# Squares added on VectorE, three pairs on x not yet normed in every layer, and output products seven pairs behind

## The chip, the core and the metric

The kernel runs on one core of a Trainium2 chip. Its time is what the device takes for one execution, in microseconds (us); 1053.85 is the median of three runs (1053.67 to 1056.78). The core has TensorE (PE, matrix products into PSUM), VectorE (DVE), ScalarE (ACT), GpSimd (POOL) and SyncE (SP, which here issues the loads of the weights).

## The reference

Two stacks of layers in float32 on a sequence of 256 positions and 1024 features. Every layer is x = x + f(norm(x)), where norm is

```
y = x32 * lax.rsqrt(jnp.mean(x32 * x32, axis=-1, keepdims=True) + EPS)
return (y * g.astype(jnp.float32)).astype(x.dtype)
```

The layers in their order: mixer0 (attention and pooling), ffn0, mixer1 (a gated linear recurrence), ffn1, mixer2 (four branches on quarters of the features: rwkv, spatial gating, a short convolution and s5, a complex diagonal recurrence), ffn2, and a last norm. ffn0 and ffn1 are

```
z = causal_dwconv(h @ w_in, conv_w, conv_b)
u, g = jnp.split(z, 2, axis=-1)
return (jax.nn.gelu(g) * u) @ w_out
```

with 2816 features in u and in g. In mixer2 and ffn2 the normed x is also scaled and shifted by factors computed from a second input.

## The kernel before

x is kept transposed in SBUF as eight tiles X[m] of 128 features by 256 positions. A weight is 128x128; each product with one takes three matmuls of 256 columns in the fp32r format, high by high, high by low and low by high (lines 281 to 283 in `mm3`, line 286 in the norm products). The weights come in chunks of 16 by SP's DMAs (`raw`). Half a chunk, eight weights or 24 matmuls, is one split: ScalarE casts the high half (`hi`, line 247) and VectorE subtracts it for the low half (`lo`, line 323). Splits are made up to four ahead, in five buffers each for hi and lo, and beyond these in slots borrowed from an arena of 46.

The order of the instructions on each engine comes from a list scheduler at build time, which takes the program's text, in three lanes, and starts what it believes ready; each engine runs its own list in order. Where the text moves a step, the scheduler may move others.

Ahead of each layer stands a norm. The last product of the layer before (`out_last`) finishes X[m] one tile after the other; `norm_add` squares each on ScalarE and adds the squares up. `norm_sum` sums over the features with two matmuls of one column and starts the reciprocal square root, some twelve tiny operations on VectorE (the tiles nv, nr...y, nr...t). `norm_spread` spreads the result over the partitions by two more matmuls, and `make_h` writes the normed tiles hs.

PE doesn't wait for that: `in_gen` starts the layer's first pairs of column tiles on x that has only the norm's gain on it (`xgh`, high, and `xgl`, low, the latter being the group s<-xp,pvt,xgh of the trace) and multiplies the result by the norm's factor afterwards. A pair is two weight columns, u and g of ffn, with eight steps of k. The function `products` issues them, and its second argument says at which of the eight steps the sum and the spread stand. Later pairs use hs.

`ffn` takes its 22 pairs from `in_gen`; `evac` of a pair has ScalarE and VectorE do the convolution, the gelu, the product and its split, and `out(k)` adds pair k's output product to X's accumulators, LAG pairs behind. The last four pairs go through `out_last`. In s5 (`s5_run`), eight parts p pass through st_a (rotation, with two adds on GpSimd), st_b (two scans and a rotation back on VectorE) and st_c (the products with C), which are taken in groups of four; PE does other branches of mixer2 between them.

Of the kernel before, what the change touches and what calls it, by code (L numbers as in the profile page):

```python
# [11 lines left out]
AF = mybir.ActivationFunctionType  # L12
OP = mybir.AluOpType
# [3 lines left out]
T = 256  # L17
# [9 lines left out]
N_CHUNK = -(-N_TILES // TPC)  # L27
N_SLOT = 46
MAGIC = 12582912.0
NORM_A, NORM_B = 4, 6  # L30
SUM_AT, SPREAD_AT = 6, 1
SB = 3
SC = 6
STEPS0 = (3, 7)
# [7 lines left out]
S5_N = 4  # L42
S5_W = (2, 5, 8)
RW_W = 1
LAG = 5
LAST = 4
LAG2 = 3
LAST2 = 2
# [89 lines left out]
class Prog:  # L138
# [226 lines left out]
    def norm_add(self, m):  # L365
        nc = self.nc
        acc = self.sacc[:, :T]
        if self.gain is not None:
            self.split_act(self.X[:, m, :], *self.xgo(m), scale=self.gain(m))
        if self.nsq == 0:  # L370
            nc.scalar.activation(acc, self.X[:, m, :], AF.Square)
        elif self.nsq < 7:
            sq = self.sqb[:, (self.nsq % 2) * T:(self.nsq % 2) * T + T]
            nc.scalar.activation(sq, self.X[:, m, :], AF.Square)  # L374
            nc.gpsimd.tensor_tensor(acc, acc, sq, op=OP.add)  # L375
        else:
            sq = self.sqb[:, T:]
            nc.scalar.activation(sq, self.X[:, m, :], AF.Square)  # L378
            self.tt(acc, acc, sq, OP.add)
        self.nsq += 1  # L380
# [421 lines left out]
    def in_gen(self, specs, hs, scaled=False):  # L802

        lead = 0 if hs else 3 if self.shift is not None else 2
        if lead:
            sh = self.shift is not None
            n = T + 2 if sh else T  # L810
            bs, o = [], []

            def products(js, at):

                for j in js:
                    b = [self.bk() for _ in range(2 if sh else 1)]
                    bs.append(b)
                    o.append([x[:, :n] for x in b] if sh else [b[0][:, :T], b[0][:, T:]])
                for q, k in enumerate(self.ORDER):
                    if q in at:  # L820
                        at[q]()
                    xh, xl = self.xgo(k, n)
                    for j in js:
                        for i, (w, m) in enumerate(specs[j]):
                            wh, wl = self.W((w, k, m))
                            self.mm(o[j][i], wh, xh, q == 0 and (sh or i == 0), False)
                            self.mm(o[j][i][:, :T], wh, xl, False, False)
                            self.mm(o[j][i], wl, xh, False, q == KD - 1)
            rbs = []

            def spread():
                rbs.append(self.norm_spread())
                if not scaled:
                    hs.extend(self.make_h(rbs[0]))
            if sh:
                products((0, 1), {SUM_AT: self.norm_sum})
                products((2,), {SPREAD_AT: spread})
            else:
                products((0, 1), {NORM_A: self.norm_sum, NORM_B: spread})
            rb = rbs[0]  # L840
            if not scaled:
                self.fr(*self.xgl)
            self.set_lead(4, self.down)
            for j in range(lead):
                z = self.al()
                if sh:
                    bias = self.cst([128, 2], f"hb{self.uid}")
                    for i in range(len(specs[j])):
                        zi = z[:, i * T:i * T + T]
                        self.tt(zi, o[j][i][:, :T], rb[:, :T], OP.mult)  # L850
                        self.nc.vector.tensor_reduce(bias[:, i:i + 1], o[j][i][:, T:n], axis=AX.X, op=OP.add)
                        self.nc.scalar.activation(zi, zi, AF.Identity, bias=bias[:, i:i + 1])
                else:
                    b = bs[j][0]
                    self.tt(z.rearrange("p (i t) -> p i t", i=2), b.rearrange("p (i t) -> p i t", i=2),
                            rb[:, :T].unsqueeze(1).to_broadcast([128, 2, T]), OP.mult)
                self.bf(*bs[j])
                if j == lead - 1 and not scaled:
                    self.fr(rb)
                yield j, z  # L860
        for j in range(lead, len(specs)):
            b = self.bk()
            for k in range(KD):
                for i, (n, m) in enumerate(specs[j]):
                    x = self.xgo(k) if scaled else self.hl(hs[k])
                    self.mm3(b[:, i * T:i * T + T], (n, k, m), x, k == 0 and i == 0, k == KD - 1)
                if k == 3:
                    self.step()
            if scaled:
                z = self.al()  # L870
                self.tt(z.rearrange("p (i t) -> p i t", i=2), b.rearrange("p (i t) -> p i t", i=2),
                        rb[:, :T].unsqueeze(1).to_broadcast([128, 2, T]), OP.mult)
                self.bf(b)
                b = z
            yield j, b
        if scaled:
            self.fr(rb, *self.xgl)


    def ffn(self, l):  # L880
# [24 lines left out]
        def out(k):  # L905
            if k == 0:
                self.acc_begin()
            self.out_k(wo, k, self.hl(ys[k]), k == 0)
            self.fr(ys.pop(k))
        for p, b in self.in_gen(specs, hs):  # L910
# [3 lines left out]
            if p == SIDE:  # L914
                self.lanes[1].append((self.rg_small, self.s5_setup)[l]())
            if p >= LAG and p - LAG < NFT - LAST:
                out(p - LAG)
        self.fr(*hs)
        if l == 1:
# [3 lines left out]
            self.ts(self.gt1h, self.mod[:, 16:24], 0.5, OP.mult)  # L923
        for k in range(NFT - LAG, NFT - LAST):
            out(k)
# [271 lines left out]
    def s5_run(self, ud):  # L1197

        nc = self.nc
# [46 lines left out]
        def st_c(ps):  # L1246


            for n, (c, q, i) in enumerate(((0, 0, 0), (1, 0, 1), (1, 1, 0), (0, 1, 1))):
                for p in ps:  # L1250
                    r = 32 * (p % 4)
                    self.mm(yb[r:r + 32, (p // 4) * T:(p // 4) * T + T], self.s5c[:, c, p, :], Y[p][q][:, i, :],
                            n == 0, n == 3)
            for p in ps:
                self.fr(*Y.pop(p))

        for s in range(8 + S5_C):
            if s >= S5_C and (s - S5_C) % S5_N == S5_N - 1:
                st_c(range(s - S5_C - S5_N + 1, s - S5_C + 1))
            if 0 <= s - 1 < 8:  # L1260
                Y[s - 1] = st_b(s - 1, V.pop(s - 1))
            if s < 8:
                V[s] = st_a(s)
            yield
            if s in S5_W:
                yield
# [725 lines left out]
```

## Time and profile before

| | |
|---|---|
| median of three runs | 1053.85 us |
| the profiled execution | 1055.76 us |
| its span | 1054.0 us, granted clock 0.988 |
| PE busy | 1022.2 us, 97% |
| VectorE busy | 865.2 us, 82% |
| ScalarE busy | 609.1 us, 58% |
| GpSimd busy | 130.2 us, 12% |
| read from HBM | 200.32 MB, 191 GB/s over the span |

A row of the timeline gives the start of an instruction, its duration, the engine, the line of the kernel, the operation, output<-inputs by the program's names, the shapes, the count where equal neighbours are drawn together, and in brackets the idle time of the engine in front and the instruction that ended it. A row of the windows gives, for a stretch of time, each engine's busy time and instruction count. The page is the summary of the whole execution.

### The profile page before, as it was taken

Reading aid. Unit: us, or ns where it says so; the run is one execution under the profiler, and the core shown is the slowest. Engines: PE = TensorE matmul, PEld = TensorE weight load, DVE = VectorE, ACT = ScalarE, POOL = GpSimd, SP = SyncE. Lnnn points to the kernel's source line nnn. Section 1 sums busy time; section 2 is a strip of 40 time slices with the busy share of each in tenths; the row PEclk is TensorE's granted clock in tenths of the full one; section 3 lists DMA queues with packets and bytes.
Section 4 is the critical chain, followed back from the end, with each engine's and each line's share of the span. In section 5 each row is a group of like instructions: output and inputs, shape, how many; then the busy total and the mean of one; then the engine's idle time right before and its main releaser. Section 6 shows DMA issues by size and latency. Waiting matters only on the chain. (4 is left out here: it accounts for less than half of the span.)

```text
span 1054.0 us, 21535 instructions
## 1 busy us (share of the span) xinstructions
PE 1022.2 (97%) x8834; PEld 988.3 (94%) x8834; DVE 865.2 (82%) x1616; ACT 609.1 (58%) x953; POOL 130.2 (12%) x128
## 2 busy tenths in 40 slices
PE   9999999999989999999999999889999999999996
PEld 8878999999989999999998999778999999999996
DVE  5887899987789989999999887998567979775553
ACT  6556665555669966665654588223335557444444
POOL 2001000000010011000394200244300220000001
PEclk9999999999999999999999999989999999999999
DMA  8952467976572183678546544224445454955531
GB/s 306 351 184 83 158 215 276 321 267 222 192 268 90 44 294 123 229 255 293 204 160 199 191 161 147 94 81 161 161 153 209 158 168 159 381 178 197 179 142 41
DMA packets 32499, 202.76 MB, mean 192 GB/s; under 512 B 3600, under 2 KB 5136, under 8 KB 9232
## 3 DMA queue, kind: packets, MB, share of 16 engines
q1 hardware_dynamic: 31392, 199.80, 53.8%
q10 hardware_dynamic: 1008, 1.58, 0.5%
q8 instruction: 69, 1.13, 0.4%
q14 instruction: 30, 0.25, 0.1%
HBM read 200.32 MB, written 1.05 MB: 191 GB/s over the span
## 5 line engine op out<-in xcount | busy, mean ns | idle before, releaser
L282 PE MATMUL b<-s,hi 128*128 128x256 f32 x2248 | 636.2, 283 | 1.7 <-DVE s L332 0.9
L281 PE MATMUL b<-s,hi 128*128 128x256 f32 x2172 | 615.8, 285 | 4.8 <-ACT s L343 2.5
L283 PE MATMUL b<-s,lo 128*128 128x256 f32 x2172 | 612.7, 283 | 1.4 <-DVE lo L323 1.4
L323 DVE TENSOR_TENSOR lo<-raw,hi 128x1024 fp32r<-128x1024 f32 (+1 forms) x311 | 391.6, 1264 | 113.5 <-ACT hi L247 113.0
L247 ACT CAST hi<-raw 128x1024 fp32r<-128x1024 f32 (+1 forms) x311 | 322.5, 1041 | 276.6 <-PE b L282 251.4
L282 PEld LDWEIGHTS b<-s,hi 128*128 128x128 f32 x2248 | 426.2, 190 | 6.2 <-issue 3.1
L281 PEld LDWEIGHTS b<-s,hi 128*128 128x128 f32 x2172 | 411.0, 190 | 12.5 <-issue 3.5
L283 PEld LDWEIGHTS b<-s,lo 128*128 128x128 f32 x2172 | 411.6, 190 | 2.9 <-DVE lo L323 1.8
L375 POOL TENSOR_TENSOR s<-s,s 128x256 f32<-128x256 f32 x42 | 38.2, 910 | 595.9 <-ACT s L374 592.8
L332 DVE SCALAR_TENSOR_TENSOR s<-b,pvt,s 128x255 f32<-128x255 f32 (+1 forms) x161 | 75.9, 476 | 2.2 <-ACT s L889 1.0
L323 DVE TENSOR_TENSOR s<-s,s 128x256 fp32r<-128x256 f32 (+3 forms) x131 | 72.3, 563 | 2.0 <-ACT s L378 0.6
L466 DVE SCALAR_TENSOR_TENSOR ada<-ada,s 128x512 f32<-128x512 f32 x96 | 63.6, 682 | 2.1 <-DMA ada<-in_ada_dram 2.1
L286 PE MATMUL b<-xgh,hi 128*128 128x258 f32 (+1 forms) x172 | 50.2, 292 | 0.0
L889 ACT ACTIVATE s<-b,pvt 128x256 f32<-128x256 f32 x80 | 43.8, 555 | 10.5 <-PE b L283 10.4
L286 PE MATMUL b<-xgh,lo 128*128 128x258 f32 (+1 forms) x172 | 49.9, 290 | 0.0
L286 PE MATMUL b<-s,hi 128*128 128x256 f32 x172 | 49.7, 289 | 0.0
L343 ACT CAST s<-s 128x256 fp32r<-128x256 f32 (+1 forms) x77 | 32.8, 439 | 27.6 <-DVE s L323 19.1
L286 PE MATMUL b<-s,s 128*32 128x256 f32 (+5 forms) x204 | 35.5, 353 | 6.3 <-DVE s L323 5.9
L323 DVE TENSOR_TENSOR s<-s 128x256 f32<-128x256 f32 (+3 forms) x70 | 35.5, 508 | 4.5 <-ACT s L1798 4.0
L286 PEld LDWEIGHTS b<-s,s 128*32 128x32 f32 (+3 forms) x204 | 21.5, 151 | 13.6 <-issue 8.2
L286 PEld LDWEIGHTS b<-s,hi 128*128 128x128 f32 x172 | 34.0, 198 | 0.0
L286 PEld LDWEIGHTS b<-xgh,lo 128*128 128x128 f32 x172 | 33.9, 197 | 0.0
(370 smaller groups left out, 1047.3 us busy)
## 6 DMA issues: line engine op xcount, KB each, us to landing
raw<-in_wst_dram SPq DMA_DIRECT2D x157, 1024.0 KB, 5.0
ada<-in_ada_dram SPq DMA_DIRECT2D x24, 1024.0 KB, 7.2
raw<-in_wst_dram SPq DMA_DIRECT2D x4, 512.0 KB, 7.0
s<-in_catt_dram SPq DMA_DIRECT2D x8, 192.0 KB, 6.9
s<-in_rgw_dram SPq DMA_DIRECT2D x5, 256.0 KB, 2.7
raw<-in_wst_dram SPq DMA_DIRECT2D x4, 256.0 KB, 5.6
xp<-in_xt_dram ACTq DMA_DIRECT2D x3, 256.0 KB, 6.4
s<-in_cinv_dram SPq DMA_DIRECT2D x2, 256.0 KB, 5.8
```

The costliest lines, as they stand in the source:

```text
L247: self.nc.scalar.copy(h, s)
L281: mm(out, wh, x[0], start=start, stop=False, skip_group_check=True)
L282: mm(out, wh, x[1], start=False, stop=False, skip_group_check=True)
L283: mm(out, wl, x[0], start=False, stop=stop, skip_group_check=True)
L286: self.nc.tensor.matmul(out, l, r, start=start, stop=stop, skip_group_check=True)
L323: self.nc.vector.tensor_tensor(out, a, b, op=op)
L332: self.nc.vector.scalar_tensor_tensor(out, a, s, b, op0=op0, op1=op1)
L343: nc.scalar.copy(hi, src)
L375: nc.gpsimd.tensor_tensor(acc, acc, sq, op=OP.add)
L466: self.nc.vector.scalar_tensor_tensor(x, x, 0.5, self.cs[h], op0=OP.mult, op1=OP.mult, accum_out=self.macc[:, h, i:i + 1])
L889: nc.scalar.activation(c[:, i, :], z, AF.Identity, scale=self.pv(f"fcw{l}2", m), bias=self.pv(f"fcb{l}", m))
```

## The change

1. `norm_add`: every square after the first is added by VectorE. Before, GpSimd added the second to the seventh, and VectorE the eighth.
2. `in_gen`: three pairs go on x not yet normed in the unshifted layers too (ffn0, mixer1, ffn1), where it was two. The sum stands at step 6 of the first two pairs and the spread at step 2 of the third; before, they stood at steps 4 and 6 of the first two. In the shifted layers (mixer2, ffn2) the spread moves from step 1 to step 2.
3. `ffn`: LAG 5 becomes 7.
4. `s5_run`: one more `yield` ahead of each group of C products.

```diff
-NORM_A, NORM_B = 4, 6
-SUM_AT, SPREAD_AT = 6, 1
+SUM_AT, SPREAD_AT = 6, 2
...
-LAG = 5
+LAG = 7
...
-        elif self.nsq < 7:
+        else:
             sq = self.sqb[:, (self.nsq % 2) * T:(self.nsq % 2) * T + T]
-            nc.scalar.activation(sq, self.X[:, m, :], AF.Square)
-            nc.gpsimd.tensor_tensor(acc, acc, sq, op=OP.add)
-        else:
-            sq = self.sqb[:, T:]
             nc.scalar.activation(sq, self.X[:, m, :], AF.Square)
             self.tt(acc, acc, sq, OP.add)
...
-        lead = 0 if hs else 3 if self.shift is not None else 2
+        lead = 0 if hs else 3
...
-            if sh:
-                products((0, 1), {SUM_AT: self.norm_sum})
-                products((2,), {SPREAD_AT: spread})
-            else:
-                products((0, 1), {NORM_A: self.norm_sum, NORM_B: spread})
+            products((0, 1), {SUM_AT: self.norm_sum})
+            products((2,), {SPREAD_AT: spread})
...
             if s >= S5_C and (s - S5_C) % S5_N == S5_N - 1:
+                yield
                 st_c(range(s - S5_C - S5_N + 1, s - S5_C + 1))
```

On PE, ahead of ffn0, the sum (b<-cb,s) stood before the change inside the products with the split hi_1185:

```order
L286 MATMUL b_130_1285<-xgh,hi_1185 128x256
L286 MATMUL b_130_1285<-s_128_1128,hi_1185 128x256
L286 MATMUL b_130_1285<-xgh,lo_1186 128x256
L286 MATMUL b_131_1344<-cb,s_123_1123 128x1 x2
L286 MATMUL b_129_1284<-xgh,hi_1185 128x256
L286 MATMUL b_129_1284<-s_125_1125,hi_1185 128x256
```

and with the change it stands here:

```order
L285 MATMUL b_130_1285<-xgh,hi_1223 128x256
L285 MATMUL b_130_1285<-s_126_1126,hi_1223 128x256
L285 MATMUL b_130_1285<-xgh,lo_1224 128x256
L285 MATMUL b_131_1374<-cb,s_123_1123 128x1 x2
L285 MATMUL b_129_1284<-xgh,hi_1223 128x256
L285 MATMUL b_129_1284<-s_127_1127,hi_1223 128x256
```

It has moved behind one more split of weights (hi_1223 follows hi_1185), 24 matmuls, the products of one step having 12. The spread follows 36 matmuls after the sum, where it followed after 32.

On VectorE, at the end of ffn1, the last pair's evacuation (s_444, and its split into s_445) and the weight splits (lo) stood in this order:

```order
L323 TENSOR_TENSOR lo_7192<-raw_7023,hi_7191 128x1024
L332 SCALAR_TENSOR_TENSOR s_444_7207<-b_443_7142,pvt,s_444_7207 128x255
L332 SCALAR_TENSOR_TENSOR s_444_7207<-b_443_7142,pvt,s_444_7207 128x254
L323 TENSOR_TENSOR lo_7232<-raw_7023,hi_7231 128x1024
L332 SCALAR_TENSOR_TENSOR s_444_7207<-b_443_7142,pvt,s_444_7207 128x255
L332 SCALAR_TENSOR_TENSOR s_444_7207<-b_443_7142,pvt,s_444_7207 128x254
L323 TENSOR_TENSOR s_444_7207<-s_444_7207 128x256
L323 TENSOR_TENSOR lo_7268<-raw_7088,hi_7267 128x1024
L323 TENSOR_TENSOR s_445_7216<-s_444_7207,s_445_7216 128x256
L323 TENSOR_TENSOR xp<-xp,b_390_5448 128x256
```

With the change, where the same pair is s_454 and s_455:

```order
L322 TENSOR_TENSOR lo_7140<-raw_6971,hi_7139 128x1024
L331 SCALAR_TENSOR_TENSOR s_454_7155<-b_453_7090,pvt,s_454_7155 128x255
L331 SCALAR_TENSOR_TENSOR s_454_7155<-b_453_7090,pvt,s_454_7155 128x254
L322 TENSOR_TENSOR lo_7180<-raw_6971,hi_7179 128x1024
L331 SCALAR_TENSOR_TENSOR s_454_7155<-b_453_7090,pvt,s_454_7155 128x255
L331 SCALAR_TENSOR_TENSOR s_454_7155<-b_453_7090,pvt,s_454_7155 128x254
L322 TENSOR_TENSOR s_454_7155<-s_454_7155 128x256
L322 TENSOR_TENSOR lo_7216<-raw_7036,hi_7215 128x1024
L322 TENSOR_TENSOR s_455_7164<-s_454_7155,s_455_7164 128x256
L322 TENSOR_TENSOR lo_7244<-raw_7036,hi_7243 128x1024
L322 TENSOR_TENSOR lo_7274<-raw_7107,hi_7273 128x1024
L322 TENSOR_TENSOR xp<-xp,b_406_5630 128x256
```

The weight splits ahead of the last split are fewer against what PE still has to do: after it, two more of them follow before X is added to (xp<-xp,b), where X followed at once.

On PE, in s5's second group, the first C products (32x256, s_564, s_568 and s_578 being the parts 4, 5 and 6) stood apart:

```order
L283 MATMUL b_589_8755<-s_471_7616,lo_8636 128x256
L286 MATMUL b_530_8341<-s_564_8554,s_387_5389 32x256
L286 MATMUL b_530_8341<-s_568_8611,s_387_5389 32x256
L281 MATMUL b_591_8832<-s_526_8300,hi_8635 128x256
L282 MATMUL b_591_8832<-s_527_8301,hi_8635 128x256
L283 MATMUL b_591_8832<-s_526_8300,lo_8636 128x256
...
L281 MATMUL b_591_8832<-s_526_8300,hi_8635 128x256
L286 MATMUL b_530_8341<-s_578_8678,s_387_5389 32x256
L282 MATMUL b_591_8832<-s_527_8301,hi_8635 128x256
```

With the change the three (s_574, s_581, s_588) stand together:

```order
L281 MATMUL b_602_8843<-s_477_7630,hi_8677 128x256
L282 MATMUL b_602_8843<-s_477_7630,lo_8678 128x256
L285 MATMUL b_540_8353<-s_574_8566,s_397_5401 32x256
L285 MATMUL b_540_8353<-s_581_8640,s_397_5401 32x256
L285 MATMUL b_540_8353<-s_588_8718,s_397_5401 32x256
L280 MATMUL b_602_8843<-s_478_7631,hi_8727 128x256
L281 MATMUL b_602_8843<-s_478_7631,hi_8727 128x256
```

Part 6's product has moved 24 to 26 matmuls to the back; those of the parts 4 and 5 come up to it. In the first group the parts 0 and 1 come up to part 2 in the same way, and part 2 stands two rows later than it did.

## Rows read from the trace of the kernel before

**Rows 1.** Page, busy time of each engine: us, share of the span, instructions
```profile
PE 1022.2 (97%) x8834; PEld 988.3 (94%) x8834; DVE 865.2 (82%) x1616; ACT 609.1 (58%) x953; POOL 130.2 (12%) x128
```

**Rows 2.** Waits of PE: us in total, times, longest us
```profile
PE b L286 <- DVE s L323: 11.8, 5, 3.0
...
PE b L283 <- DVE lo L323: 1.4, 2, 1.0
```

**Rows 3.** Busy time by stretch; us, PE PEld DVE ACT POOL, then PEclk, DMA share, GB/s
```profile
120.00:185.00 65.00, 65.00 (x550) 64.91 (x550) 64.77 (x161) 42.44 (x69) 0.00 (x0) 1.00 0.62 219
...
410.00:515.00 105.00, 104.85 (x887) 104.65 (x887) 104.25 (x260) 66.97 (x105) 0.54 (x3) 1.00 0.67 235
580.00:590.00 10.00, 10.00 (x78) 10.00 (x78) 8.12 (x12) 6.52 (x13) 3.12 (x4) 0.89 0.33 112
```

**Rows 4.** Timeline of PE at the three sums: start, us, [idle before <-releaser]
```profile
108.31 0.28 PE L286 MATMUL b<-s,hi 128*128 128x256 f32 x1
108.43 0.28 PE L286 MATMUL b<-xgh,lo 128*128 128x256 f32 x1
110.42 0.58 PE L286 MATMUL b<-cb,s 128*128 128x1 f32 x4 [1.71 <-DVE s L323]
...
111.25 0.42 PE L286 MATMUL b<-xgh,lo 128*128 128x256 f32 x1
111.46 0.42 PE L286 MATMUL b<-xgh,hi 128*128 128x256 f32 x1
...
114.59 0.28 PE L286 MATMUL b<-xgh,hi 128*128 128x256 f32 x1
...
305.26 0.70 PE L286 MATMUL b<-cb,s 128*128 128x1 f32 x4 [2.77 <-DVE s L323]
...
402.43 0.58 PE L286 MATMUL b<-cb,s 128*128 128x1 f32 x4 [1.48 <-DVE s L323]
```

**Rows 5.** Timeline of DVE at the norm ahead of ffn0
```profile
97.51 2.25 DVE L332 SCALAR_TENSOR_TENSOR s<-xp,pvt,xgh 128x256 fp32r<-128x256 f32 x3
...
101.48 0.96 DVE L332 SCALAR_TENSOR_TENSOR s<-xp,pvt,xgh 128x256 fp32r<-128x256 f32 x1
102.36 1.76 DVE L323 TENSOR_TENSOR lo<-raw,hi 128x1024 fp32r<-128x1024 f32 x1
104.05 0.47 DVE L332 SCALAR_TENSOR_TENSOR s<-xp,pvt,xgh 128x256 fp32r<-128x256 f32 x1
...
106.24 1.84 DVE L332 SCALAR_TENSOR_TENSOR s<-xp,pvt,xgh 128x256 fp32r<-128x256 f32 x2
...
109.87 0.41 DVE L323 TENSOR_TENSOR s<-s,s 128x256 f32<-128x256 f32 x1
110.23 1.22 DVE L323 TENSOR_TENSOR lo<-raw,hi 128x1024 fp32r<-128x1024 f32 x1
```

**Rows 6.** Page, the squares' adds on GpSimd: xcount | busy, mean ns | idle before
```profile
L375 POOL TENSOR_TENSOR s<-s,s 128x256 f32<-128x256 f32 x42 | 38.2, 910 | 595.9 <-ACT s L374 592.8
```

**Rows 7.** Timeline of PE at ffn1's end
```profile
577.46 0.39 PE L281 MATMUL b<-s,hi 128*128 128x256 f32 x1 [1.65 <-ACT s L343]
578.49 0.42 PE L282 MATMUL b<-s,hi 128*128 128x256 f32 x1 [0.65 <-DVE s L323]
```

**Rows 8.** Timeline of DVE at the same place
```profile
578.02 0.42 DVE L323 TENSOR_TENSOR s<-s,s 128x256 fp32r<-128x256 f32 x1
```

**Rows 9.** Timeline of PE in s5, at the two late C products
```profile
684.03 0.59 PE L286 MATMUL b<-s,s 128*32 128x256 f32 x2 [3.04 <-DVE s L323]
...
708.15 0.79 PE L286 MATMUL b<-s,s 128*32 128x256 f32 x2 [2.81 <-DVE s L323]
```

**Rows 10.** Timeline of DVE in s5, two scans that follow each other
```profile
705.31 1.78 DVE L1238 TENSOR_TENSOR_SCAN s<-s5mag,s 128x256 f32<-128x256 f32 x2 [0.63 <-POOL s L1229]
...
711.30 1.78 DVE L1238 TENSOR_TENSOR_SCAN s<-s5mag,s 128x256 f32<-128x256 f32 x2
```

**Rows 11.** Timeline of PE at the spread ahead of ffn2
```profile
872.08 0.49 PE L286 MATMUL b<-cb,nr709y 128*128 128x128 f32 x2 [0.98 <-DVE nr709y L332]
```

## The prediction

> **What bounds the kernel now.** I read the page first [rows 1]: TensorE (PE) is busy for 1022.2 of 1054.0 us, VectorE (DVE) for 865.2. A matmul of 256 columns starts every 0.12 us when nothing is late (108.31, 108.43 in [rows 4]), so the matmuls are the floor, and a change can win only where PE stands still or runs at a lower clock. PE's waits come next [rows 2]: 11.8 us of them are five waits for one operation of VectorE, while the low halves of split weights (lo) cost 1.4 us in all. The timeline says where these are: the norm's sum of squares ahead of the first feed-forward layer (ffn0), of mixer1 and of ffn1 [rows 4], and two C products in s5 [rows 9]. Two more waits stand at ffn1's end [rows 7] and one at ffn2's spread [rows 11].
>
> Most of these waits cost more than themselves. Behind the 1.71 us at 110.42, matmuls start 0.21 us apart (111.25, 111.46) instead of 0.12, until 114.59 [rows 4]: the half clock, 1.2 for 2.4 GHz. 16 matmuls take 3.34 us there instead of 1.9, so the dip costs about 1.5 us with the two matmuls before. The granted clock of 0.89 behind ffn1's end [rows 3] shows one more. I price a dip at 1.5 us wherever a wait of 1.7 us or more goes, and none for the 1.48 at 402.43, behind which the stretch of 410 to 515 us has a clock of 1.00.
>
> Last comes VectorE where the sums wait for it [rows 5]. The split of the gained x (s<-xp,pvt,xgh) takes 0.47 us alone (104.05), and 0.96 (101.48) while GpSimd adds squares; a lo takes 1.22 alone (110.23) and 1.76 beside such an add (102.36). Over the six adds ahead of ffn0 that is 2.25 for some 1.27 in the three at 97.51, 0.49 at 101.48, 0.54 at 102.36 and 1.84 for some 0.87 in the two at 106.24: 3.0 us that VectorE loses to GpSimd. So it is VectorE, itself held up by GpSimd, that the sum waits for.
>
> **The change part by part.** *Squares on VectorE.* 42 adds of 0.91 us leave GpSimd [rows 6], and 42 come to VectorE. One such add takes 0.41 us, 0.36 from start to start (109.87 to 110.23) [rows 5]; I take 0.34 in a dense run, so 2.0 us a norm. Against 3.0 us of stretching that goes, VectorE has 1.0 us less to do ahead of a sum (0.9 taken) in the five norms with xgl; the first and the last norm have no such splits and gain nothing there. I cost those two at 0 (between +1 and −1 us): the first starts among the loads, and the last trades six adds of 0.91 for shorter ones just before the end. Each add stands behind its square on ScalarE; the xgl split of about half a us before it in VectorE's queue covers most of that wait, and what is queued behind an add is the next lo.
>
> The Trainium skill (SBUF — State Buffer, "Who interferes with whom") says that a VectorE instruction with two inputs in SBUF and a GpSimd instruction that reads SBUF exclude each other for the whole instruction. The trace agrees that they collide, but the stretch is about 0.5 us an instruction, not the 0.91 us of an add. By the rule the six adds would cost up to 5.5 us, and VectorE would gain 3.5 a norm; the sum would change by mixer1's 0.2 alone, since the other waits at the sums are gone by either. The skill (Perfetto Trace Analysis, "Optimizing Scalar/DVE Operations") also advises offloading a saturated VectorE, even to GpSimd, which is the reverse of this edit, while warning that the two share a port. Here the warning fits the rows better than the advice; what the advice would make of it is the last rival.
>
> *Late sum, three pairs.* In the order for PE the sum stands 24 matmuls later in ffn0 and ffn1, 2.8 us at 0.118 each, and 13 later in mixer1, 1.5 us. With 0.9 less on VectorE, ffn0's wait of 1.71 goes (3.7 us of room against 1.7), and its dip: −3.2. ffn1's 1.48 goes: −1.5. Mixer1's 2.77 is met by 1.5 + 0.9 = 2.4, so 0.2 to 0.4 may stay, too short for a dip: 2.77 + 1.5 − 0.2 = −4.1. What is late next is the spread: it stands 36 matmuls behind the sum in ffn0 and ffn1, 4.2 us, and 60 in mixer1, 7.1 us. The chain between is one short add, some eleven tiny operations and a lo, about 4.5 us in ffn0 from the sum's end, against 4.7 with the sum itself; up to 0.5 us may be late, which goes to the new waits below. For mixer2 and ffn2 the spread stands 4 to 7 matmuls later: ffn2's wait of 0.98 [rows 11] loses 0.8 by that and 0.9 by VectorE: −0.7 taken, between −1.0 and 0.
>
> *Seven pairs behind.* At ffn1's end PE waits 1.65 us for a split on ScalarE and 0.65 for the low half made by VectorE at 578.02 [rows 7, 8], the last pair's evacuation, and runs at half clock behind it. With two more pairs of output products held back, VectorE's order has this evacuation two weight splits earlier against the weights that PE needs then. 1.65 + 0.65 + 1.5 = 3.8; I leave 0.5 of wait: −3.3 (between −3.8 and −1).
>
> What the same edit costs is at the layers' start. Two further pairs of 48 matmuls (5.7 us) pass without output products between them, so evacuations, z of the third pair and make_h come denser on VectorE, which is already busy 64.77 of 65 us in ffn0 and 104.25 of 105 in ffn1, with PE without a stop [rows 3]. No row shows how far the lo splits are ahead. Bounds: 0, if the lead of four splits covers it, and all that PE wins in the two layers less what VectorE wins, 3.2 + 1.5 + 3.3 − 1.8 = 6.2, if VectorE is exactly even. I take 3.0, the middle.
>
> *s5.* The extra yield holds the first C products of a group back until the third is there too, but in PE's order only the sixth part's C moves (some 25 matmuls, 3 us); the one PE waits 3.04 us for at 684.03 [rows 9] stands where it stood, as does VectorE's order ahead of it. The second wait, 2.81 at 708.15, goes: PE comes there 24 matmuls later, near 708.2. But the eighth part's C stands 28 matmuls behind it, near 711.5, and the 24 short matmuls of rwkv that stood ahead of it now stand behind it, while VectorE's scans come every 6.0 us (705.31, 711.30) [rows 10], whatever PE does. The sixth part's C began 2.84 us after its scan, so the eighth's can begin near 714.1. The wait moves and keeps its dip: 2.6 new for 2.81, −0.2. Ends: +1, and −8.8, if both waits and dips go (3.04 + 2.81 + 3.0).
>
> Sum: −3.2 − 4.1 − 1.5 − 0.7 − 3.3 + 3.0 − 0.2 = −10.0 us. Against the profiled execution (span 1054.0, 1.76 around it, 1055.76 us) that is 1045.8; the median of the runs shown is 1.91 below that execution, so 1043.9, and I forecast 1044.
>
> **Rivals.** *All of it goes.* The yield in s5 works as it reads, and the lead covers the feed-forward layers: −10.0 − 8.6 − 3.0 = −21.6 at most, about 1032. For it: the lo waits are only 1.4 us [rows 2]. Against: the order, in which the wait of 684.03 keeps its place. With half of the 11.6 it would be 1038, and the middle of the two is 1035.
>
> *VectorE is the floor in the feed-forward layers.* The waits at the sums are then only the first place where its lateness shows; PE, earlier by what they cost, catches up with the lo splits and hs a few us later. For it: 99% busy in both stretches [rows 3]. Against: it loses 3.0 us a norm to GpSimd only while GpSimd adds. With 6.2 instead of 3.0 returned, one dip a layer and the spreads late by 0.5 each, the gain is −10.0 + 3.2 + 3.0 + 1.0 = −2.8: 1051.
>
> *Slower: the slots.* Two more pairs of feed-forward outputs alive take slots of the arena from which the weight splits borrow when their five buffers are out. If each of the 22 pairs of either layer then waits 0.4 us for a lo, 44 × 0.4 = 17.6 goes back, and with the 3.0 replaced by it the sum is −10.0 − 3.0 + 17.6 = +4.6: 1058. The point from which it decides is a wait of 0.3 us a pair. For it: VectorE has no room to catch up there. Against: at the layer's end the splits stand singly between the evacuations, as they did before.
>
> *The edit of the squares does not do what it says.* If the stretching came from ScalarE's work and not from GpSimd, VectorE would have 2.0 more instead of 1.0 less ahead of each sum. ffn0 would still be met (2.8 against 1.7 + 2.0, wait 0.9, no dip), mixer1 not (2.77 + 2.0 − 1.5 = 3.3 with its dip), ffn1 with 0.7 left (1.48 + 2.0 − 2.8): −10.0 + 0.9 + 4.6 + 0.7 + 2.0 in the later stretch = −1.8, 1052. Against it: splits without GpSimd beside them, such as 104.05, are at 0.47 among the same work of ScalarE.
>
> **How the numbers follow.** A measurement of this kernel can tell 0.3%, 3.2 us, from no change. The forecast (1040 to 1048) has 0.58, everything gone (1032 to 1040) 0.16, VectorE as the floor (1048 to 1054) 0.14, the squares' failure (1050 to 1054) 0.05, the slots 0.07. Faster than 1050.7: the first two and some three fifths of the third, 0.83. Slower than 1057: most of the slots, 0.06. Between: 0.11. The range of 1034 to 1052 leaves out the slots, the lower edge of everything gone and the upper one of the two in between.
>
> **What would show it.** GpSimd's L375 rows gone and every xgl split at 0.47 us; no wait above 0.5 at the sums of ffn0, mixer1 and ffn1, and clock 1.00 in their stretches; the last evacuation of ffn1 without its wait; at s5 one C product still 3 us late near its first place and one at the eighth part. I am wrong if lo waits of PE grow beyond 3 us (the floor or the slots), if xgl splits stay near 0.96, or if s5 no longer waits.

## The result, and the profile after

The changed kernel takes 1042.85 us (median of 4 runs, 1040.94 to 1046.05) against 1054.78 for the kernel before in the same runs; the ratio is 0.9889 with a 95% interval of 0.9873 to 0.9906, or some 11.7 us. The forecast was 1044, 10.0 us less than before. The profiled execution of the changed kernel is its slowest, 1046.05 us with a span of 1044.3, so 9.7 us of the change can be read in the traces. Line numbers are 1 to 9 lower in the changed kernel: 322 and 331 are VectorE's 323 and 332 of before, 280 to 282 the three matmuls, 285 those of the norm.

The page's busy times, which answer [rows 1]:

```profile
PE 1015.2 (97%) x8834; PEld 980.9 (94%) x8834; DVE 865.7 (83%) x1662; ACT 605.3 (58%) x953; POOL 96.8 (9%) x86
```

VectorE executes 46 instructions more and is busy as long as before: what it took over is paid by what no longer holds it up. PE is busy 7.0 us less with the same 8834 matmuls, and that is clock. The waits of PE, with us in total, times and the longest, answer [rows 2]:

```profile
PE b L285 <- DVE s L322: 7.4, 3, 3.0
PE b L282 <- DVE lo L322: 4.0, 5, 1.3
PE b L280 <- ACT s L342: 3.0, 3, 1.1
```

Three of the five long waits for VectorE are left or new, all in s5; the waits for lo have grown from 1.4 to 4.0 us. The timeline of PE at the sums ahead of ffn0 and mixer1, at its longest waits in ffn0 and ffn1 and at its waits in s5, in order of time (two more waits for lo, 0.40 and 0.41, stand in ffn1 at 418.19 and 488.02):

```profile
109.39 0.50 PE L285 MATMUL b<-cb,s 128*128 128x1 f32 x4
...
159.90 0.38 PE L282 MATMUL b<-s,lo 128*128 128x256 f32 x1 [1.31 <-DVE lo L322]
...
299.88 0.61 PE L285 MATMUL b<-cb,s 128*128 128x1 f32 x4
...
484.54 0.38 PE L282 MATMUL b<-s,lo 128*128 128x256 f32 x1 [0.89 <-DVE lo L322]
...
568.85 0.38 PE L280 MATMUL b<-s,hi 128*128 128x256 f32 x1 [1.01 <-ACT s L342]
569.88 0.38 PE L281 MATMUL b<-s,hi 128*128 128x256 f32 x1 [0.65 <-DVE s L322]
...
674.46 0.59 PE L285 MATMUL b<-s,s 128*32 128x256 f32 x2 [3.01 <-DVE s L322]
...
699.79 0.59 PE L285 MATMUL b<-s,s 128*32 128x256 f32 x2 [2.12 <-DVE s L322]
...
705.81 3.51 PE L285 MATMUL b<-s,s 128*32 128x256 f32 x26 [2.27 <-DVE s L322]
```

The sums have no bracket any more: no wait in front. Added up over every wait of 0.25 us or more, PE stands still for 23.9 us in the trace of before and 21.2 in that of after. Only 2.7 us of the 9.7 are standing time; the rest is the half clock behind the waits. The windows of before, each 5 us behind a wait (columns as in [rows 3], the clock third from the end):

```profile
62.00:67.00 5.00, 4.13 (x20) 3.78 (x20) 4.09 (x15) 1.78 (x6) 0.00 (x0) 0.66 0.37 146
110.00:115.00 5.00, 4.58 (x26) 4.61 (x27) 3.67 (x14) 1.25 (x2) 0.00 (x0) 0.66 0.61 210
305.00:310.00 5.00, 4.74 (x27) 4.74 (x28) 4.42 (x13) 1.26 (x3) 0.00 (x0) 0.66 0.82 262
578.00:583.00 5.00, 4.51 (x25) 4.51 (x26) 2.90 (x6) 1.76 (x3) 0.00 (x0) 0.66 0.59 198
```

and the same places in the changed kernel, then the two stretches of half clock in s5, where the kernel before has two as well:

```profile
62.00:67.00 5.00, 4.36 (x32) 3.85 (x33) 4.86 (x19) 2.94 (x10) 0.00 (x0) 1.00 0.28 107
108.00:113.00 5.00, 5.00 (x45) 5.00 (x44) 4.26 (x14) 2.10 (x2) 0.00 (x0) 1.00 0.82 275
301.00:306.00 5.00, 5.00 (x44) 5.00 (x43) 4.89 (x12) 2.35 (x4) 0.00 (x0) 1.00 0.98 359
569.00:574.00 5.00, 4.35 (x36) 4.15 (x37) 5.00 (x8) 4.14 (x6) 0.00 (x0) 1.00 0.74 282
674.00:679.00 5.00, 4.54 (x23) 4.16 (x24) 4.37 (x7) 0.60 (x1) 2.27 (x2) 0.66 0.23 56
705.00:710.00 5.00, 4.19 (x32) 2.23 (x33) 5.00 (x8) 0.18 (x1) 2.19 (x1) 0.66 0.37 100
```

Four stretches of half clock are gone, some 1.5 us each. One of them, at 62 us, has the same waits in front of it in both traces, and is luck (see the last section). On VectorE, the norm ahead of ffn0 now reads so, against [rows 5]:

```profile
100.35 0.48 DVE L331 SCALAR_TENSOR_TENSOR s<-xp,pvt,xgh 128x256 fp32r<-128x256 f32 x1
100.75 0.42 DVE L322 TENSOR_TENSOR s<-s,s 128x256 f32<-128x256 f32 x1
101.08 0.48 DVE L331 SCALAR_TENSOR_TENSOR s<-xp,pvt,xgh 128x256 fp32r<-128x256 f32 x1
101.48 0.42 DVE L322 TENSOR_TENSOR s<-s,s 128x256 f32<-128x256 f32 x1
```

Splits at 0.48, adds at 0.42, and 0.33 us from an add to the next start: the sum of six is the 2.0 us that was predicted.

One more view of the traces says in which layer the time went. PE's matmuls number 700, 2300, 3080, 4722 and 7342 (counted from 0) are the same ones in every run, with the same neighbours, and stand at the five norms' sums or up to 66 matmuls ahead of them. From the start of one to the start of the next, in us, one profiled execution each:

| | before | changed | `no_yield` | `sq_only` | `no_lead` | `lag5` |
|---|---|---|---|---|---|---|
| ffn0 | 193.4 | 191.3 | 190.0 | 191.7 | 191.5 | 190.0 |
| mixer1 | 101.2 | 96.5 | 96.5 | 96.9 | 97.1 | 99.5 |
| ffn1 | 200.7 | 199.3 | 197.9 | 198.9 | 194.9 | 202.0 |
| mixer2 | 267.7 | 268.4 | 267.7 | 267.3 | 267.1 | 267.2 |

The runs named here are told below; `no_yield` has the changed kernel's order of instructions up to s5, so its first three rows are a second execution of them.

### The profile page after: what moved, and what is told of

The parts are those of the page before. It is cut to its first block, busy times and chain, and to the rows that moved or that the text cites. A ratio compares the mean times of both kernels' runs of the same rounds, so it can differ in the third digit from the quotient of the medians.

```text
span 1044.3 us, 21508 instructions
## 1 busy us (share of the span) xinstructions
PE 1015.2 (97%) x8834; PEld 980.9 (94%) x8834; DVE 865.7 (83%) x1662; ACT 605.3 (58%) x953; POOL 96.8 (9%) x86
## 5 line engine op out<-in xcount | busy, mean ns | idle before, releaser
L281 PE MATMUL b<-s,hi 128*128 128x256 f32 x2192 | 616.9, 282 | 1.8 <-DVE s L331 0.9
L280 PE MATMUL b<-s,hi 128*128 128x256 f32 x2128 | 600.6, 283 | 4.8 <-ACT s L342 3.0
L282 PE MATMUL b<-s,lo 128*128 128x256 f32 x2128 | 598.2, 282 | 4.1 <-DVE lo L322 4.0
L281 PEld LDWEIGHTS b<-s,hi 128*128 128x128 f32 x2192 | 413.4, 189 | 6.0 <-issue 3.0
L280 PEld LDWEIGHTS b<-s,hi 128*128 128x128 f32 x2128 | 400.6, 189 | 12.2 <-issue 4.0
L282 PEld LDWEIGHTS b<-s,lo 128*128 128x128 f32 x2128 | 400.9, 189 | 6.8 <-DVE lo L322 5.8
L322 DVE TENSOR_TENSOR s<-s,s 128x256 f32<-128x256 f32 (+3 forms) x173 | 89.2, 524 | 8.0 <-ACT s L373 3.7
L285 PE MATMUL b<-xgh,hi 128*128 128x256 f32 (+1 forms) x212 | 60.5, 285 | 0.0
L285 PE MATMUL b<-s,hi 128*128 128x256 f32 x212 | 59.6, 281 | 0.0
L285 PE MATMUL b<-xgh,lo 128*128 128x256 f32 (+1 forms) x212 | 59.6, 281 | 0.0
L285 PE MATMUL b<-s,s 128*128 128x256 f32 (+5 forms) x212 | 39.2, 380 | 7.9 <-DVE s L322 7.4
L285 PEld LDWEIGHTS b<-s,hi 128*128 128x128 f32 x212 | 40.1, 189 | 0.0
L285 PEld LDWEIGHTS b<-xgh,lo 128*128 128x128 f32 x212 | 40.0, 189 | 0.0
L285 PEld LDWEIGHTS b<-xgh,hi 128*128 128x128 f32 x212 | 39.9, 188 | 0.0
```

What stands on the lines that cost most here:

```text
L280: mm(out, wh, x[0], start=start, stop=False, skip_group_check=True)
L281: mm(out, wh, x[1], start=False, stop=False, skip_group_check=True)
L282: mm(out, wl, x[0], start=False, stop=stop, skip_group_check=True)
L285: self.nc.tensor.matmul(out, l, r, start=start, stop=stop, skip_group_check=True)
L322: self.nc.vector.tensor_tensor(out, a, b, op=op)
```

## The experiments

Each was run beside the kernel before on one chip, but not all on the same one, so the ratios, which are all to the kernel before, are compared and not the times.

**Each part alone.** `sq_only` has the squares on VectorE and nothing else:

```diff
-        elif self.nsq < 7:
+        else:
             sq = self.sqb[:, (self.nsq % 2) * T:(self.nsq % 2) * T + T]
-            nc.scalar.activation(sq, self.X[:, m, :], AF.Square)
-            nc.gpsimd.tensor_tensor(acc, acc, sq, op=OP.add)
-        else:
-            sq = self.sqb[:, T:]
             nc.scalar.activation(sq, self.X[:, m, :], AF.Square)
             self.tt(acc, acc, sq, OP.add)
```

> The kernel before with the squares added on VectorE and nothing else of the change. Theory: GpSimd's adds stretch VectorE by 3.0 us a norm and the adds there cost 2.0, so VectorE is 0.9 earlier at the five sums; the list scheduler also puts ffn0's sum 8 matmuls (0.9 us) and mixer1's 17 (2.0) later by itself. ffn0: 1.71 gone with its dip (-3.2); mixer1: 2.77 gone with its dip (-4.2); ffn1: 1.48 to 0.6 (-0.9); ffn2's spread -0.9. About -9 us, 0.991 to 0.993. Rival (the late sum and third pair carry the gain): -0 to -3 us. Rival (the stretching is not GpSimd's): slower by 5 or more.

Measured: 1046.41 us, 0.9925 (0.9912 to 0.9938). No sum waits: the timeline of PE has no bracket at ffn0's, mixer1's and ffn1's sums, and none at ffn2's spread; ffn1's end waits 1.59 + 0.65 as before. The theory holds, with ffn1's sum better than expected (0.6) and two new waits of 0.35 and 0.82 at ffn0's spread and hs. In the listing by form the xgl splits (x16: those with the gain from pvt that the trace draws in one group) are first in before, then in `sq_only`:

```profile
L332 DVE SCALAR_TENSOR_TENSOR s<-xp,pvt,xgh 128x256 fp32r<-128x256 f32 x16 | 12.4, 809 | 0.0
```

```profile
L332 DVE SCALAR_TENSOR_TENSOR s<-xp,pvt,xgh 128x256 fp32r<-128x256 f32 x16 | 7.5, 481 | 0.2 <-ACT xgh L337 0.2
```

`lead_only` has the third pair, the late sum and the later spread:

```diff
-SUM_AT, SPREAD_AT = 6, 1
+SUM_AT, SPREAD_AT = 6, 2
...
-        lead = 0 if hs else 3 if self.shift is not None else 2
+        lead = 0 if hs else 3
...
-            if sh:
-                products((0, 1), {SUM_AT: self.norm_sum})
-                products((2,), {SPREAD_AT: spread})
-            else:
-                products((0, 1), {NORM_A: self.norm_sum, NORM_B: spread})
+            products((0, 1), {SUM_AT: self.norm_sum})
+            products((2,), {SPREAD_AT: spread})
```

> The kernel before with the third pair, the late sum and the later spread alone: squares on GpSimd, LAG 5, no extra yield. Theory after the runs so far (VectorE's work sets the pace of the feed-forward layers, and a wait that the late sum removes comes back behind it): ffn0's and ffn1's waits at the sums go, but at ffn1's end PE waits more than the 1.65 + 0.65 of the kernel before, 3 us or more, and mixer1's sum still waits 1 to 2; within 2 us of the kernel before, 0.998 to 1.001. Rival (the prediction's reading, the late sum wins the waits at ffn0 and ffn1 and a dip): 4 to 6 us faster, 0.994 to 0.996.

Measured: 1051.52 us, 0.9970 (0.9960 to 0.9980): 3.2 us, between the two, with an interval that reaches the edge of either. The mechanism of the first shows in PE's timeline. The sums of ffn0 and ffn1 wait no more, mixer1's waits 1.19, and ffn1's end waits longer than in [rows 7]:

```profile
301.46 0.61 PE L286 MATMUL b<-cb,s 128*128 128x1 f32 x4 [1.19 <-DVE s L323]
...
571.98 0.39 PE L281 MATMUL b<-s,hi 128*128 128x256 f32 x1 [3.38 <-ACT s L343]
573.01 0.58 PE L282 MATMUL b<-s,hi 128*128 128x256 f32 x1 [0.65 <-DVE s L323]
```

The wait at ffn1's end is 1.7 us longer than in the kernel before, with half clock for 6.8 us behind it.

`lag7_only` has the lag:

```diff
-LAG = 5
+LAG = 7
```

> The kernel before with LAG 7 and nothing else of the change. Theory (the lag takes the last evacuations of a feed-forward layer out of the way, whatever stands at its start): at ffn1's end 1.65 + 0.65 us fall to at most 0.65 and the dip goes, 2.5 to 3.2 us; the sums of ffn0 and ffn1 wait 1.7 and 1.5 as before, mixer1's less than 2.77. 2 to 5 us faster than the kernel before, 0.995 to 0.998. Rival (the lag pays only where VectorE has been freed of something else): within 1 us, the wait at ffn1's end or for lo as long as before.

Measured: 1051.05 us, 0.9964 (0.9952 to 0.9976). At ffn1's end there is no wait of 0.25 us left and no dip: 3.8 us by the ratio (2.5 to 5.1), which is the prediction's 1.65 + 0.65 + 1.5. The sums wait 1.71, 2.77 and 1.49, all three as before; that mixer1's would fall was wrong.

**Each part undone.** `no_sq`, `no_lead` and `lag5` are the changed kernel with the first, the second or the third of these diffs turned back (squares, third pair, lag); in `no_lead` the shifted layers keep their later spread, and the unshifted ones have the sum and spread at steps 4 and 6. `no_yield` is the changed kernel with this:

```diff
             if s >= S5_C and (s - S5_C) % S5_N == S5_N - 1:
-                yield
                 st_c(range(s - S5_C - S5_N + 1, s - S5_C + 1))
```

> The whole change but with the squares on GpSimd as before. Theory: the sums stand 24, 13 and 24 matmuls later than in the kernel before, so ffn0 and ffn1 are without a wait, mixer1 keeps 2.77 - 1.5 = 1.3 us, perhaps with a dip; xgl splits at 0.96 us; VectorE 0.9 us later in each of ffn0, mixer1, ffn1, mixer2, ffn2, of which a part shows as waits for lo. 2 to 5 us slower than the changed kernel: 0.991 to 0.994 of the kernel before. Rival (the squares carry the gain): within 3 us of the kernel before, 0.997 or more.

Measured: 1049.33 us, 0.9953 (0.9937 to 0.9969), 6.7 us slower than the changed kernel by the ratios, more than the 2 to 5 expected. Mixer1's sum waits 0.84 and its spread 1.55, and a lo at 487.64 1.38. Without the squares the rest of the change wins less than half as much; the result lies between the expectation and its rival.

> The whole change without its third pair in the unshifted layers; their sum and spread at steps 4 and 6 of the two pairs. Theory: with the squares on VectorE alone no sum waited, since the scheduler puts the sums later by itself; ffn0's spread and hs wait 0.3 to 1.2 us. 0.5 to 2 us slower than the changed kernel, 0.989 to 0.992 of the kernel before. Rival (the third pair and the late sum are needed): waits at two or three sums again, 4 us or more slower, 0.993.

Measured: 1042.36 us, 0.9877 (0.9864 to 0.9890), which can't be told from the changed kernel (0.9873 to 0.9906). The sums don't wait: with VectorE's adds in the text, the scheduler's order has ffn0's sum 8 rows and mixer1's 13 rows later than in the kernel before, with two pairs only. What the missing pair costs stands behind, at ffn0's spread and hs:

```profile
114.68 0.57 PE L285 MATMUL b<-cb,nr132y 128*128 128x128 f32 x3 [0.36 <-DVE nr132y L331]
...
116.78 0.62 PE L280 MATMUL b<-s,hi 128*128 128x256 f32 x3 [0.83 <-ACT s L342]
```

and the lo waits of the changed kernel in the two layers and both waits at ffn1's end are gone. So ffn1 is 3.0 us shorter than in `no_yield`, and ffn0 and mixer1 are 1.5 and 0.6 us longer (the table above).

> The whole change with LAG 5 as before. Theory: at ffn1's end 1.6 + 0.65 us and a dip come back where the changed kernel has 1.0 + 0.65 without one (+2 us), and the lo waits inside the two layers (1.3, 0.4, 0.9, 0.4 in the changed kernel) go by half (-1.5): within 2 us of the changed kernel, 0.988 to 0.991. Rival (the longer lag is what wins): 4 us or more slower, 0.993. Rival (the longer lag is what costs): 3 us faster, 0.986.

Measured: 1047.94 us, 0.9935 (0.9920 to 0.9950), 4.8 us slower than the changed kernel: the rival that the longer lag wins. Expected were 1.6 + 0.65 us at ffn1's end; PE waits 3.38 + 0.47 there, the wait of `lead_only`, with a dip, and 1.46 at mixer1's sum. The lo waits inside the two layers are not halved, as expected, but gone: no wait for lo of 0.25 us or more is left there.

> The whole change without the extra yield in s5. Theory: waits of 3.0 and 2.8 us at the two C products with a dip each, as before, against 3.0, 2.1 and 2.3 in the changed kernel; the time is that of the changed kernel within 1 us, 0.988 to 0.990 of the kernel before. Rival (the yield wins what it was made for): 3 us or more slower than the changed kernel, 0.992.

Measured: 1044.56 us, 0.9915 (0.9901 to 0.9928). That is 2.7 us slower than the changed kernel by the ratios, with intervals that overlap, so whether the yield gains anything isn't settled by the time. The traces show no gain: mixer2 takes 267.7 us here, as in the kernel before, and 268.4 in the changed kernel. The waits are 3.07, 1.11 and 2.83 against 3.01, 2.12 and 2.27, 7.0 and 7.4 us: the yield moves waits within s5.

**Two yields.** `y2` is the changed kernel with one more:

```diff
             if s >= S5_C and (s - S5_C) % S5_N == S5_N - 1:
                 yield
+                yield
                 st_c(range(s - S5_C - S5_N + 1, s - S5_C + 1))
```

> The whole change with two extra yields ahead of each group of C products instead of one. In the order for PE the third part's C then stands 24 matmuls (2.8 us) later than in the changed kernel, and the sixth's and eighth's 36 and 11. Theory: PE's wait at these products is only VectorE's lateness, so 3.0 falls to 0.2 and 2.1 to 0, with both dips, the eighth part keeps 1 to 2 us: 4 to 8 us faster than the changed kernel, 0.982 to 0.985 of the kernel before. Rival (VectorE and GpSimd are the floor of this stretch and PE only waits elsewhere): within 1.5 us of the changed kernel, the waits at a later product.

Measured: 1044.32 us, 0.9902 (0.9889 to 0.9915), the rival's result. The three waits have become two at later products, 4.01 at 679.30 and 3.45 at 705.56, 7.5 us against the changed kernel's 7.4, and mixer2 takes 268.8 us. What PE does first in s5 doesn't matter; what VectorE has ready does.

**Is it GpSimd that stretches VectorE?** `pool_idle` is the changed kernel with adds on GpSimd that nobody reads:

```diff
             nc.scalar.activation(sq, self.X[:, m, :], AF.Square)
+            if self.nsq < 7:
+                nc.gpsimd.tensor_tensor(self.sacc[:, T:], sq, sq, op=OP.add)
             self.tt(acc, acc, sq, OP.add)
```

> The changed kernel, and beside each of the six squares of a norm one more add on GpSimd (128x256, the square to itself, into an unused half of a tile), whose result nobody reads. Theory (GpSimd's adds stretch VectorE's instructions that run beside them): the xgl splits go from 0.47 to about 0.96 us again, VectorE has 2 to 3 us more ahead of each of the five sums, and waits come back at mixer1's sum (about 2.5 us with a dip), less at ffn0 and ffn1, and for lo behind: 5 to 9 us slower than the changed kernel, 0.994 to 0.997 of the kernel before. Rival (the stretching came from what waits for the adds, or from ScalarE): within 1.5 us of the changed kernel, splits at 0.47.

Measured: 1054.85 us, 0.9998 (0.9987 to 1.0009): 42 adds of 0.85 us, on an engine that is idle for nine tenths of the time, cost 11.5 us, everything that the change had won and more than expected. This is the cleanest of the runs: PE, VectorE and ScalarE execute the changed kernel's instructions in the changed kernel's order, one for one, so no move of the scheduler has a part in it. VectorE is busy for 878.1 us instead of 865.7. The profiled execution took 1051.76 us at a granted clock of 0.997, the other eleven had 0.988 to 0.995. So the traces show 5.7 of the 11.5 us, nearly all of it standing time of PE (26.5 us against 21.2); the lower clock of the others was not traced. VectorE's timeline at the norm ahead of ffn0, then the two GpSimd adds that run beside its first two rows:

```profile
102.02 0.83 DVE L331 SCALAR_TENSOR_TENSOR s<-xp,pvt,xgh 128x256 fp32r<-128x256 f32 x1
102.78 0.83 DVE L322 TENSOR_TENSOR s<-s,s 128x256 f32<-128x256 f32 x1
103.53 0.47 DVE L331 SCALAR_TENSOR_TENSOR s<-xp,pvt,xgh 128x256 fp32r<-128x256 f32 x1
103.93 0.41 DVE L322 TENSOR_TENSOR s<-s,s 128x256 f32<-128x256 f32 x1
```

```profile
101.63 0.94 POOL L375 TENSOR_TENSOR s<-s 128x256 f32<-128x256 f32 x1 [3.48 <-ACT s L373]
...
102.65 0.67 POOL L375 TENSOR_TENSOR s<-s 128x256 f32<-128x256 f32 x1
```

While GpSimd adds (101.63 to 103.32), a split and an add take 0.83 us each, and right after 0.47 and 0.41. The added instructions wait for ScalarE's squares alone, and only the next square into the same half waits for them (1.2 us in all, at the last norm), so no data passes from them to VectorE. Mixer1's sum waits 2.09 again, ffn2's 1.61 and mixer2's spread 1.51.

**The same idea elsewhere.** `s5_dve` is the changed kernel with s5's two adds on VectorE:

```diff
-            nc.gpsimd.tensor_tensor(m1[:, 0, :], m1[:, 0, :], m2[:, 1, :], op=OP.add)
-            nc.gpsimd.tensor_tensor(m1[:, 1, :], m1[:, 1, :], m2[:, 0, :], op=OP.subtract)
+            self.tt(m1[:, 0, :], m1[:, 0, :], m2[:, 1, :], OP.add)
+            self.tt(m1[:, 1, :], m1[:, 1, :], m2[:, 0, :], OP.subtract)
```

> The changed kernel with the two adds of s5's rotation (lines 1220 and 1221) on VectorE too. In the changed kernel a part takes 6.0 us of VectorE, of which 0.63 is a wait for GpSimd and about 0.5 a scan stretched beside GpSimd's second add. Theory (VectorE, held up by GpSimd, sets the end of this stretch): the two adds cost 0.7, so a part takes about 5.5 us, eight parts 3 to 4 us less; the scans go from 0.86 to 0.6 each, the C products' waits of 3.0, 2.1 and 2.3 fall by 3 to 4 together: 2 to 5 us faster than the changed kernel, 0.984 to 0.987 of the kernel before. Rival (VectorE has no room and gains nothing): the same within 1.5 us or slower.

Measured: 1039.44 us, 0.9847 (0.9832 to 0.9862), 4.4 us faster than the changed kernel, as the theory had it. The scans by form, in the changed kernel and then in `s5_dve` (busy us, mean ns, idle before):

```profile
L1229 DVE TENSOR_TENSOR_SCAN s<-s5mag,s 128x256 f32<-128x256 f32 x16 | 12.7, 836 | 3.3 <-POOL s L1220 2.5 <-POOL s L1221 0.7
```

```profile
L1229 DVE TENSOR_TENSOR_SCAN s<-s5mag,s 128x256 f32<-128x256 f32 x16 | 10.4, 694 | 0.0
```

The C products wait 0.96 and 0.64 us instead of 3.01, 2.12 and 2.27; 2.74 us come back at 717.73 in rwkv, where the changed kernel waits 0.70: the VectorE instruction that PE waits for there took 1.74 us beside GpSimd, for 0.68 in the changed kernel, and the two weight splits behind it took 4.50. Mixer2 takes 262.2 us.

`best1` is `no_lead` with the edit of `s5_dve`; `best2` is `best1` with the lines 1302, 1470, 1471, 1485 and 1737 (masks and sums of mixer2) on VectorE in the same way:

```diff
-        nc.gpsimd.tensor_tensor(ws, ws, tr, op=OP.mult)
+        self.tt(ws, ws, tr, OP.mult)
...
-        nc.gpsimd.tensor_tensor(XT, TT, bc(mk[:, 192:256], 8), op=OP.mult)
-        nc.gpsimd.tensor_tensor(XT, XT, bc(i2, 8), op=OP.add)
+        self.tt(XT, TT, bc(mk[:, 192:256], 8), OP.mult)
+        self.tt(XT, XT, bc(i2, 8), OP.add)
...
-            nc.gpsimd.tensor_tensor(TM, TT, bc(lm, 8), op=OP.mult)
+            self.tt(TM, TT, bc(lm, 8), OP.mult)
...
-                    nc.gpsimd.tensor_tensor(self.merged[q], self.merged[q], th, op=OP.add)
+                    self.tt(self.merged[q], self.merged[q], th, OP.add)
```

> The changed kernel without its third pair in the unshifted layers and with the two adds of s5's rotation on VectorE: squares, LAG 7, yield and s5 adds. Theory: the two edits act in different layers and add up; the third pair wins nothing. 0.983 to 0.986 of the kernel before, 1037 to 1040 us. Rival (no third pair costs once s5 is shorter, or s5's gain was a luckier order): 0.988 or more.

Measured: 1037.83 us, 0.9846 (0.9832 to 0.9859), as expected.

> As best1, and the other GpSimd operations of mixer2 (lines 1302, 1470, 1471, 1485 and 1737, 16 of 128x512) on VectorE too. In s5_dve PE waits 2.74 us for VectorE at 717.7, where two weight splits beside three such operations took 4.50 us instead of 2.35. Theory (GpSimd stretches VectorE there too): 16 operations cost VectorE 0.6 to 0.7 us each, 10 us over a stretch of 160 us in which it has idle time, and that wait goes; 1 to 4 us faster than best1, 0.980 to 0.984. Rival (VectorE has no room left there, and the rwkv chain gets longer): 1 us or more slower than best1.

Measured: 1032.12 us, 0.9793 (0.9780 to 0.9806), better than expected: 5.6 us faster than `best1` by the ratios and some 10 faster than the changed kernel. Its busy times and its longest waits of PE:

```profile
PE 1012.4 (98%) x8834; PEld 978.8 (95%) x8834; DVE 863.8 (84%) x1690; ACT 610.2 (59%) x953; POOL 47.0 (5%) x54
```

```profile
PE b L280 <- ACT s L342: 2.8, 3, 1.0
PE b L285 <- DVE eps L508: 1.2, 1, 1.2
PE b L285 <- DVE s L322: 1.2, 2, 1.0
```

VectorE has 74 instructions more than in the kernel before and is busy 1.4 us less. The waits of 0.25 us or more add up to 9.2 us, the only stretch of half clock is at the very end, and mixer2 takes 258.0 us.

## Why the prediction was right

The time (1044 against 1042.85, or −10.0 us against −11.7 by the ratio) and the mechanism of its first part stand, but one step got credit that belongs to another, and luck has a share in the profiled sum: some 1.5 us of it are a dip at 62 us, which no term had.

*Squares on VectorE.* Right, and larger than priced. Six adds at 0.33 us and 3.0 us of stretching that goes are in the trace; `pool_idle` shows the cause, `sq_only` the worth: 7.9 us alone. I had priced the edit by what VectorE gains at each sum, 0.9 us, and left out that the scheduler moves the sums by itself when the adds change engine (ffn0's by 8 rows, mixer1's by 17 in `sq_only`). The rival that the stretching came from ScalarE is dead: in `sq_only` ScalarE has the same work and the splits take 0.48. The Trainium skill (SBUF — State Buffer, "SBUF: two separate sides") has a VectorE instruction with two SBUF inputs and a GpSimd instruction that reads SBUF exclude each other: the one that starts first keeps the ports that they share for its whole instruction, and the other is blocked. The traces agree, and the prediction misread them when it set a stretch of 0.5 us against a whole add of 0.91: VectorE's instruction starts when part of the add is over, and only the rest of it can block. In the five norms with xgl, in the kernel before and in `pool_idle`, every VectorE instruction with both inputs in SBUF that started during one of these adds took longer by what was left of the add, less 0.13 to 0.20 us; one that had started before the add lost nothing, and the add took longer (0.94 us at 101.63 in `pool_idle`, where a lo was under way, for 0.61 at best). In the lines of `pool_idle` above, 0.55 us were left each time, and the split grew by 0.36 and the add by 0.42. An addition of PE's result to X at 1037.83 in the kernel before, with one input in PSUM, started with 0.40 us of an add left and took 0.48 us, as without one.

*Late sum, three pairs.* The step that failed. The waits at the sums and the spread go as predicted (1.71, 2.77, 1.48 and 0.98 to nothing; 0.2 was left for mixer1), but the squares alone do that too, and undoing this part costs nothing that the times can tell. Alone it wins 3.2 us and leaves ffn1's end 1.7 us worse. In company its gains and costs cancel: `no_yield` with it against `no_lead` without it has ffn0 1.5 and mixer1 0.6 us shorter and ffn1 3.0 us longer. VectorE as the floor of the feed-forward layers was therefore half right, for this part alone.

The new waits of 3.0 that I put to the lag are the four lo waits of the profiled execution (1.31, 0.40, 0.89 and 0.41). They need both parts: they are gone in `no_lead`, with the longer lag and two pairs, and in `lag5`, with three pairs and the shorter lag. That they add up to 3.0 is luck, and so is it that a sign of being wrong, lo waits beyond 3 us, showed (4.0 in all, 2.1 in `no_yield`). In `no_yield` and `y2`, which execute the same instructions in the same order up to s5, they are 0.39, 0.40, 0.33 and 0.40, 0.40, 0.25. The 1.31 follows a load of weights that came late to ScalarE in this one execution; `s5_dve`, alike up to there, has the same instruction 1.1 us earlier and no such wait. First the changed kernel, then `s5_dve`:

```profile
153.74 1.05 ACT L246 CAST hi<-raw 128x1024 fp32r<-128x1024 f32 x1 [3.02 <-DMA raw<-in_wst_dram]
```

```profile
152.63 1.05 ACT L246 CAST hi<-raw 128x1024 fp32r<-128x1024 f32 x1 [1.86 <-DMA raw<-in_wst_dram]
```

*Seven pairs behind.* The mechanism and the full term were right: 3.8 us alone, 4.8 in company (`lag5`), for 3.8 with 0.5 taken off. I left 0.5 us of wait at ffn1's end; in the profiled execution there are 1.01 + 0.65, without a dip, and since `no_lead` has neither, that rest belongs to the third pair. The slots, the slower rival, don't show: no series of lo waits in either layer.

*s5.* The term was mis-sized. The wait of 684.03 kept its place (3.01) and a new one stands at the second group's end (2.27; 2.6 was predicted), but the sixth part's wait is still 2.12, where I had it gone: 7.4 us of waits for 5.9 before, +1.5 instead of −0.2, with two dips as before. And what PE loses there hardly counts. The kernel before has 5.9 us of these waits and two dips, `no_yield` 7.0 us and one dip, and mixer2 takes 267.7 us in both. VectorE is the limit there, held up by GpSimd: with its work changed, in `s5_dve` and `best2`, the layer takes 262.2 and 258.0. I saw that for the norms in the same trace and didn't carry it to s5, where 2.5 us of idle time behind GpSimd and scans of 0.87 us (0.69 in `s5_dve`) stood in the listing of before.

*Clock.* Three dips were priced and four went. Standing time fell by 2.7 us only, so the dips carried most of the profiled 9.7; a sum over waits alone would have missed by two thirds.

## What to carry to other kernels

Work on an engine that is busy for 12% can hold up the one that sets the pace: look in the timeline for the same instruction with and without the idle engine at work beside it, and add up the difference before calling work on that engine free. Test an edit both ways, alone and undone, since a part that wins alone can be worth nothing in company. When a wait goes, look for it at the layer's end, and price the clock behind it as well as the wait where PE sets the pace; where another engine does, neither counts. Before a wait in one trace is put down to an edit, look for it in a second execution of the same instructions.

## What was not expected of the hardware

The half clock doesn't follow from the length of the wait. Ahead of the first C product in s5, PE stood still for 3.01 us in the changed kernel and was at half clock behind it (0.66 in the window of 674 to 679 above); in `no_yield` it stood still for 3.07 us at the same product and kept the full clock:

```profile
672.90:677.90 5.00, 4.89 (x34) 3.92 (x34) 4.37 (x7) 2.10 (x2) 2.28 (x2) 1.00 0.26 66
```

At 62 us, waits of 0.62 and 0.87 us led to it in the kernel before and not in the changed one, where they were 0.62 and 0.88. One dip costs about 1.5 us where PE sets the pace, and single executions of one program can differ by it: `lag5` took 1051.86 us at a clock of 0.987 and 1047.08 at 0.993. It isn't all: the changed kernel's four lie 5.1 us apart at 0.995 to 0.996, and what parts them is open, since only one of them was profiled.
